# An MLP kernel on one Trainium2 core: w2 casts pinned behind the last GELU, x casts moved, output copies put on ScalarE

## The chip, the cores and the metric

The kernel runs on one core of one Trainium2 chip. The metric is the device time of one execution, in microseconds (us).

Engine names in the profile: PE is TensorE, DVE is VectorE, ACT is ScalarE, POOL is GpSimd, SP is SyncE. A name with q at its end, such as SPq, is the queue of that engine from which DMAs are issued. "L137" is line 137 of the kernel's file. `ps` is a bank, one of the eight buffers into which TensorE accumulates; `tmp` is a temporary on its way out or to VectorE. The DMA share is the mean busy share of the core's 16 DMA engines.

## The reference

```python
x: 8 x 1024 x 1024, w1: 1024 x 4096, w2: 4096 x 1024, all float32
h = x @ w1
h = 0.5 * h * (1 + np.tanh(np.sqrt(2 / np.pi) * (h + 0.044715 * h ** 3)))
return (h @ w2).astype(np.float32)
```

## The kernel before

The 8192 tokens go through in eight superblocks of 1024. Each superblock does two products: `matmul1` with w1 and the GELU, then `matmul2` with w2. Both use a scheme that needs seven block products instead of eight, so that sums of weight blocks are wanted as operands. Operands are 16 bits wide, the inputs are float32 in DRAM.

The first superblock is different from the others, because nothing is prepared yet:

- It loads w1 and w2 in float32 through four staging buffers (`gc`), 512 KB each, 64 loads in all. ScalarE or GpSimd casts each of them to 16 bits, and only then is the buffer free for the next load.
- It keeps the cast w1 blocks in DRAM (`raw_d`). In the second superblock these are loaded again, VectorE makes the sums of w1 from them, and the sums are written to DRAM (`w1_d`) for superblocks three to eight.
- Its second product is done plainly with eight block products (512 matmuls, `matmul2_first`), in two halves of output columns (`b`), each of four quarters (`q`) with four casts (`j`, `a`). Meanwhile VectorE makes the sums of w2 and SyncE writes them to DRAM (`w2_d`), 28 writes of 512 KB.
- The x of the next superblock is cast by DMA from DRAM to DRAM (`x_cast`, on GpSimd's queue), then loaded with a transpose (on SyncE's queue).

SyncE's queue keeps its DMAs in the order of the program (`load_in_order`). On other engines a compile-time scheduler chooses the order. Each engine then runs its instructions in that order. The code is cut, and the comments at the pools are added:

```python
    up = ctx.enter_context(tc.tile_pool(name="up", bufs=26))     # 16-bit operands, "u"
    gcp = ctx.enter_context(tc.tile_pool(name="gcp", bufs=4))    # float32 staging, "gc"
    tp = ctx.enter_context(tc.tile_pool(name="tp", bufs=10))     # temporaries, "tmp"
    pp = ctx.enter_context(tc.tile_pool(name="pp", bufs=8, space=bass.MemoryType.PSUM))
    # ... cut ...
    def cast_in(dst, src, cast):
        st = gcp.tile([P] + list(dst.shape[1:]), F32, name="gc")
        load_in_order(st, src)
        cast(out=dst, in_=st)
    # ... cut: matmul1, with
        def gelu(b, c, src):
            nc.scalar.activation(out=g[b][:, c, :], in_=src, func=GELU)
    # ... cut: in matmul2_first
        for b in range(2):
            banks = [psum() for _ in range(2 * NQ)]
            # ... cut ...
            for q in range(NI // QC):
                raw = raw_units(QC, OH, (b + 1,))
                for j in range(0, QC, 2):
                    c = q * QC + j
                    for a in range(2):
                        cast_in(
                            raw[f"{a + 1}{b + 1}"][:, j:j + 2, :],
                            w2v[b, a, :, c:c + 2, :],
                            pool_copy if b == 0 and q < 2 else nc.scalar.copy,
                        )
                # ... cut: the matmuls of this quarter ...
                if b == 0:
                    keep.append(raw)
                    if q == 0:
                        keep_w1()
                    elif q == 1:
                        xb = x_cast(1, pool_last[0])
                else:
                    # ... cut: the sums of w2 ...
                    if q in (1, 2):
                        write(q - 1)
            if b == 1:
                blocks = x_transpose(xb, load_in_order)
                write(2)
                write(3)
            for i in range(2 * NQ):
                for c in range(NI - TAIL, NI):
                    mm(i, c, ready[c])
                o = temp()
                if i % 2:
                    nc.scalar.copy(out=o, in_=banks[i])
                else:
                    nc.vector.tensor_copy(out=o, in_=banks[i])
                last = store(sb, f"{i // NQ + 1}{b + 1}", i % NQ, o)
```

Of the kernel before, what the change touches and what calls it, by code (L numbers as in the profile page):

```python
# [11 lines left out]
GELU = mybir.ActivationFunctionType.Gelu_apprx_tanh  # L12
# [41 lines left out]
def kernel(  # L54
# [7 lines left out]
    nc = tc.nc  # L62
# [34 lines left out]
    def psum():  # L97
        return pp.tile([P, HT], F32, name="ps")

    def temp():  # L100
        return tp.tile([P, HT], F32, name="tmp")

    def unit(rows, cols):
        return up.tile([P, rows, cols], DT, name="u")

    def tt(out, in0, in1, op):
        nc.vector.tensor_tensor(out=out, in0=in0, in1=in1, op=op)  # L107

    def flat(t):
        return t.rearrange("p a b -> p (a b)")  # L110
# [3 lines left out]
    def load_in_order(out, in_, **kw):  # L114
        return tc.keep_in_program_order(nc.sync.dma_start(out=out, in_=in_, **kw))  # L115
# [8 lines left out]
    def make_sum(ops, m, raw, rows, cols, sl=slice(None)):  # L124

        u, op, v = B_TERMS[m]
        if op is None:
            ops[m] = raw[u]
            return
        if m not in ops:  # L130
            ops[m] = unit(rows, cols)
        tt(ops[m][:, :, sl], raw[u][:, :, sl], raw[v][:, :, sl], op)

    def cast_in(dst, src, cast):
        st = gcp.tile([P] + list(dst.shape[1:]), F32, name="gc")
        load_in_order(st, src)
        cast(out=dst, in_=st)  # L137

    def raw_units(rows, cols, bs=(1, 2)):
        return {f"{a}{b}": unit(rows, cols) for b in bs for a in (2, 1)}  # L140
# [53 lines left out]
    def load_ops(d, ms, rows, cols):  # L194
        ops = {}
        for m in ms:
            t = unit(rows, cols)
            nc.sync.dma_start(out=flat(t), in_=d[:, m - 1, :])
            ops[m] = t
        return ops  # L200
# [70 lines left out]
    def matmul1(xs, sb):  # L271
        g = {b: gp.tile([P, NI, HT], GT, name=f"g{b}") for b in ("11", "12", "21", "22")}

        def product(bank, w, m, first, last):
            ops, cs = w
            for k in range(KH):
                nc.tensor.matmul(  # L277
                    bank,
                    lhsT=ops[m][:, k, cs],
                    rhs=xs[m][:, k, :],  # L280
                    start=(first and k == 0),
                    stop=(k == KH - 1),
                    skip_group_check=not first,
                )

        def gelu(b, c, src):
            nc.scalar.activation(out=g[b][:, c, :], in_=src, func=GELU)  # L287

        late = None

        def finish(c, w, q, s2):
            product(q, w, 6, False, True)
            c22 = temp()
            tt(c22, q, s2, ADD)
            gelu("22", c, c22)

        quads = []

        def ahead(q, step):

            if q == NI // QC:
                return
            if sb > 1:
                if step == 0:
                    quads.append(load_ops(w1_d[q], (4, 5, 1, 2, 3, 7, 6), KH, QW))
                return
            if step == 0:
                quad = MadeQuad(q, sb == 0)
                quads.append(quad)
                if sb == 0:  # L310
                    quad.load()
                    quads[q - 1].keep_raw()
            for m in ((), (4,), (1, 3), (7, 6))[step]:
                quads[q].sum(m)
            if sb == 1 and step == 3:
                quads[q].copy_plain()

        if sb == 0:
            quads.append(MadeQuad(0, True))
            xs.make(5)  # L320
            cs = quads[0].load_cols(0, 1)
            quads[0].sum(4, cs)
            for m in (1, 3, 7, 6):
                if m != 3:
                    xs.make(m)
                quads[0].sum(m, cs)
            for c, n in ((1, 1), (2, 2)):
                cs = quads[0].load_cols(c, n)
                for m in SUMS:
                    quads[0].sum(m, cs)  # L330
        else:
            for step in range(QC):
                ahead(0, step)

        for c in range(NI):
            q, j = divmod(c, QC)
            if j == 0:
                ahead(q + 1, 0)
            w = (quads[q] if sb > 1 else quads[q].ops, slice(j * P, (j + 1) * P))
            pb, qb = psum(), psum()  # L340
            product(pb, w, 4, True, False)
            v = temp()
            nc.scalar.copy(out=v, in_=pb)  # L343
            product(qb, w, 5, True, False)
            u = temp()
            tt(u, v, qb, SUB)
            if late is not None:
                finish(*late)
            rb = psum()
            product(rb, w, 1, True, False)  # L350
            s = temp()
            tt(s, u, rb, ADD)
            product(pb, w, 2, False, True)
            gelu("21", c, pb)
            s2 = temp()
            tt(s2, s, pb, SUB)
            product(qb, w, 3, False, False)
            gelu("12", c, qb)
            product(rb, w, 7, False, True)
            c11 = temp()  # L360
            tt(c11, u, rb, ADD)
            gelu("11", c, c11)
            late = (c, w, qb, s2)
            if j:
                ahead(q + 1, j)
        finish(*late)
        return g, quads[-1]
# [9 lines left out]
    def matmul2_first(sb, g, keep_w1):  # L377


        TAIL = 3  # L380
        keep = []
        made = []
        blocks = None

        def write(q):
            for m in SUMS + PLAIN:
                load_in_order(w2_d[q][:, m - 1, :], flat(made[q][m]))

        for b in range(2):
            banks = [psum() for _ in range(2 * NQ)]  # L390
            ready = []

            def mm(i, c, w):
                for a in range(2):
                    nc.tensor.matmul(  # L395
                        banks[i],
                        lhsT=g[f"{i // NQ + 1}{a + 1}"][:, c, (i % NQ) * P:(i % NQ + 1) * P],
                        rhs=w[a],
                        start=(c == 0 and a == 0),
                        stop=(c == NI - 1 and a == 1),  # L400
# [7 lines that stand above are left out]
                        cast_in(  # L408
                            raw[f"{a + 1}{b + 1}"][:, j:j + 2, :],
                            w2v[b, a, :, c:c + 2, :],  # L410
                            pool_copy if b == 0 and q < 2 else nc.scalar.copy,
                        )
                for j in range(QC):
                    w = [raw[f"{a + 1}{b + 1}"][:, j, :] for a in range(2)]
                    ready.append(w)
                    if q * QC + j < NI - TAIL:
                        for i in range(2 * NQ):
                            mm(i, q * QC + j, w)
                if b == 0:
                    keep.append(raw)  # L420
                    if q == 0:
                        keep_w1()
                    elif q == 1:
                        xb = x_cast(1, pool_last[0])
                else:
                    ops = {}
                    for m in SUMS + PLAIN:
                        make_sum(ops, m, {**keep[q], **raw}, QC, OH)
                    made.append(ops)
# [7 lines that stand above are left out]
                for c in range(NI - TAIL, NI):  # L437
                    mm(i, c, ready[c])
                o = temp()
                if i % 2:  # L440
                    nc.scalar.copy(out=o, in_=banks[i])  # L441
                else:
                    nc.vector.tensor_copy(out=o, in_=banks[i])  # L443
                last = store(sb, f"{i // NQ + 1}{b + 1}", i % NQ, o)
        return last, blocks

# [58 lines left out]
    for sb in range(NSB):  # L505
        g, quad = matmul1(xs, sb)
# [39 lines left out]
```

## Time and profile before

| | before |
|---|---|
| time, median of 3 runs | 1606.53 us |
| TensorE busy | 1578.2 of 1603.7 us |
| first superblock's 960 matmuls on TensorE | 18.3 to 245.7 us |
| any later half superblock | 448 matmuls in 96.69 us |
| DMA busy share, 0 to 246 us | 0.98 |

These are lines of the profile's page of the kernel before: TensorE's busy time, then the busy tenths of TensorE and of the DMA engines and the GB/s that they moved in 40 equal slices of the span (40 us each), and the chain of work that ended last.

```profile
PE 1578.2 (98%) x7296; PEld 717.9 (45%) x7296; DVE 819.6 (51%) x1047; ACT 472.3 (29%) x784; POOL 132.1 (8%) x228
...
PE   7989999999999999999999999999999999999999
...
DMA  9999998674566646546574565746557464544511
GB/s 306 345 316 361 276 397 280 179 288 146 197 188 184 236 171 228 157 153 262 186 221 144 169 238 197 227 131 226 201 203 246 102 265 158 210 157 178 216 53 53
...
PE 95%; DMA 3%; DVE 1%; ACT 1%; issue 0%; SPq 0%; POOL 0%; DVEq 0%
```

TensorE is nearly always busy. In the first six slices, the first superblock, the DMA engines are full as well (9 means 90% or more). After that they are about half busy. The kernel thus has two stages with different limits: in the first, two resources are full at once.

TensorE's waits over 1 us that the change aims at, in the view of waits (what waited, for whom, total us, times, longest us):

```profile
PE ps L277 <- ACT g_216 L287: 7.7, 2, 7.4
...
PE ps L395 <- DVE tmp L443: 3.3, 1, 3.3
```

The first lies at 115.8 to 123.2 us, before the end of the first product. The timeline of ScalarE shows its cause (start, duration, instruction, and in brackets the idle time before it and what ended that):

```profile
110.19 0.58 ACT L343 COPY tmp<-ps 128x512 f32<-128x512 f32 x1
118.76 1.04 ACT L137 CAST u<-gc 128x1024 f16<-128x1024 f32 x1 [8.00 <-DMA gc<-in_w_dram]
...
121.56 0.62 ACT L287 ACTIVATE g_218<-tmp 128x512 bf16<-128x512 f32 x1
...
122.56 0.59 ACT L287 ACTIVATE g_216<-ps 128x512 bf16<-128x512 f32 x1
```

ScalarE stands 8.00 us before a cast of w2 whose load has not landed, and the GELUs queue behind that cast. The second product starts on TensorE at 130.34 us. The second wait is before 191.7 us, at the boundary of the column halves; VectorE's timeline shows it:

```profile
189.80 1.23 DVE L107 TENSOR_TENSOR u<-u 128x2048 f16<-128x2048 f16 x1 [7.20 <-DMA u<-xb]
190.95 0.68 DVE L443 COPY tmp<-ps 128x512 f32<-128x512 f32 x1
```

An output copy (L443) stands behind a sum that waits 7.20 us for the transposed x. TensorE needs the bank that this copy frees.

The timeline of SyncE's load queue (x20 is a run of twenty DMAs, the second column how long the issuing took):

```profile
89.33 44.96 SPq L115 DMA_DIRECT2D gc<-in_w_dram  x20
134.34 7.31 SPq L115 DMA_DIRECT2D w_d_85<-u  x7
...
160.05 26.67 SPq L115 DMA_TRANSPOSE u<-xb  x16
...
202.99 4.79 SPq L152 DMA_DIRECT2D u<-raw_d_81  x4
```

w2 loads go out until 134, then the writes of w2's sums, loads, the transposes of x (27 us), and at 202.99 the reload of w1 for the second superblock. VectorE's timeline has the first sum of that reload at 213.41; TensorE's first matmul of the second superblock comes at 245.73, 32 us later.

```profile
213.41 7.09 DVE L107 TENSOR_TENSOR u<-u 128x2048 f16<-128x2048 f16 x6 [17.25 <-DMA u<-raw_d_81]
```

Last, busy time by engine in three windows, with the granted clock, the DMA share and GB/s as the last three columns:

```profile
85.00:125.00 40.00, 32.59 (x148) 14.55 (x147) 18.82 (x27) 20.59 (x33) 13.18 (x16) 0.93 0.98 317
105.00:124.00 19.00, 11.59 (x53) 5.05 (x51) 5.48 (x9) 9.87 (x15) 2.58 (x6) 0.88 1.00 285
0.00:246.00 246.00, 224.40 (x1026) 104.40 (x1027) 135.45 (x168) 94.25 (x140) 48.42 (x69) 0.97 0.98 332
```

### The profile page before, as it was taken

The page shows a single profiled execution, that of the slowest core. Times are in us where ns is not written, and L with a number is a line of the kernel's source. Part 1 is how long each engine was busy: PE and PEld are TensorE (multiplying, and loading weights), DVE is VectorE, ACT ScalarE, POOL GpSimd, SP SyncE. Part 2 cuts the span into 40 slices and gives each one's busy share as a digit, 9 for nine tenths or more (in the row PEclk, how much of TensorE's full clock was granted, in tenths as well). Part 3 has the DMA queues.
Part 4 walks back from the last instruction along what each step waited for, and adds up shares of the span by engine and source line. Part 5 has one row for each costly group of instructions (what it writes and reads, how often), then busy time and mean ns, then how long its engine had stood idle before and what let it go on. Part 6 is the DMA issues. An engine that isn't in the chain of part 4 may idle for free.

```text
span 1603.7 us, 18985 instructions
## 1 busy us (share of the span) xinstructions
PE 1578.2 (98%) x7296; PEld 717.9 (45%) x7296; DVE 819.6 (51%) x1047; ACT 472.3 (29%) x784; POOL 132.1 (8%) x228
## 2 busy tenths in 40 slices
PE   7989999999999999999999999999999999999999
PEld 4434444444444444444444444444444444444444
DVE  6855336644455444555445554456534555455433
ACT  4645104431044210441114410244103431044310
POOL 2230113001100012000120000100001000000000
PEclk9999999999999999999999999999999999999999
DMA  9999998674566646546574565746557464544511
GB/s 306 345 316 361 276 397 280 179 288 146 197 188 184 236 171 228 157 153 262 186 221 144 169 238 197 227 131 226 201 203 246 102 265 158 210 157 178 216 53 53
DMA packets 161820, 338.91 MB, mean 211 GB/s; under 512 B 72257, under 2 KB 78401, under 8 KB 160833
## 3 DMA queue, kind: packets, MB, share of 16 engines
q1 hardware_dynamic: 146944, 278.97, 50.4%
q0 software_dynamic: 14784, 58.73, 11.5%
q8 instruction: 57, 0.93, 0.2%
q14 instruction: 35, 0.28, 0.1%
HBM read 266.34 MB, written 85.98 MB: 220 GB/s over the span
## 4 chain that ended last, share of the span: by engine, by line
PE 95%; DMA 3%; DVE 1%; ACT 1%; issue 0%; SPq 0%; POOL 0%; DVEq 0%
PE ps L277 46%; PE ps L461 42%; PE ps L395 7%; DMA gc<-in_w_dram 2%; DVE u L107 1%; ACT u L137 0%; DVE tmp L107 0%; DMA u<-in_x_dram 0%; DMA u<-xb 0%; SPq L115 0%; POOL u L118 0%; ACT g_218 L287 0%; ACT g_216 L287 0%; ACT g_217 L287 0%; ACT tmp L343 0%
## 5 line engine op out<-in xcount | busy, mean ns | idle before, releaser
L277 PE MATMUL ps<-u 128*128 128x512 f16 x3584 | 779.8, 380 | 13.1 <-ACT g_216 L287 7.7
L107 DVE TENSOR_TENSOR tmp<-tmp,ps 128x512 f32<-128x512 f32 x652 | 447.1, 687 | 661.6 <-PE ps L461 333.3
L277 PEld LDWEIGHTS <-u 128*128 128x128 f16 x3584 | 351.1, 98 | 440.3 <-issue 15.9
L461 PE MATMUL ps<-u,gc 128*128 128x512 f16 x2240 | 485.7, 379 | 0.0
L461 PEld LDWEIGHTS <-gc 128*128 128x128 bf16 x2240 | 219.2, 98 | 264.3
L375 POOL DMA_DIRECT2D out_dram<-tmp x112 | 60.6, 542 | 1108.0 <-ACT tmp L481 733.9
L107 DVE TENSOR_TENSOR u<-u 128x2048 f16<-128x2048 f16 (+2 forms) x110 | 123.0, 1152 | 56.6 <-ACT u L137 21.5
L343 ACT COPY tmp<-ps 128x512 f32<-128x512 f32 x128 | 73.0, 570 | 258.2 <-PE ps L277 258.2
L107 DVE TENSOR_TENSOR tmp<-ps,tmp 128x512 f32<-128x512 f32 x128 | 88.4, 691 | 5.9 <-PE ps L277 1.2
L481 ACT COPY tmp<-ps 128x512 f32<-128x512 f32 x28 | 16.4, 586 | 177.3 <-PE ps L461 177.3
L395 PE MATMUL ps<-u,g_217 128*128 128x512 f16 x128 | 49.0, 383 | 3.3 <-DVE tmp L443 3.3
L395 PE MATMUL ps<-u,g_218 128*128 128x512 f16 x128 | 49.0, 383 | 0.0
L395 PE MATMUL ps<-u,g_215 128*128 128x512 f16 x128 | 48.9, 382 | 0.0
L395 PE MATMUL ps<-u,g_216 128*128 128x512 f16 x128 | 48.8, 381 | 0.0
L137 ACT CAST u<-gc 128x1024 f16<-128x1024 f32 x36 | 37.2, 1044 | 37.6 <-DMA gc<-in_w_dram 37.6
L487 ACT COPY tmp<-ps 128x512 f32<-128x512 f32 x28 | 16.4, 586 | 80.3 <-PE ps L461 80.3
L475 ACT COPY tmp<-ps 128x512 f32<-128x512 f32 x28 | 16.4, 586 | 74.9 <-PE ps L461 74.9
L118 POOL CAST u<-gc 128x1024 f16<-128x1024 f32 (+1 forms) x26 | 28.5, 1105 | 73.8 <-DMA gc<-in_w_dram 60.0
L254 POOL DMA_DIRECT2D xb<-in_x_dram x56 | 27.5, 509 | 18.1 <-DMA out_dram<-tmp 14.5
L441 ACT COPY tmp<-ps 128x512 f32<-128x512 f32 x8 | 4.7, 586 | 71.1 <-PE ps L395 71.1
L395 PEld LDWEIGHTS <-g_218 128*128 128x128 bf16 x128 | 12.6, 98 | 18.8 <-issue 3.9
L395 PEld LDWEIGHTS <-g_215 128*128 128x128 bf16 x128 | 12.6, 99 | 15.5 <-issue 0.8
(120 smaller groups left out, 848.8 us busy)
## 6 DMA issues: line engine op xcount, KB each, us to landing
gc<-in_w_dram SPq DMA_DIRECT2D x64, 512.0 KB, 6.8
out_dram<-tmp POOLq DMA_DIRECT2D x112, 256.0 KB, 4.4
u<-w_d_85 SPq DMA_DIRECT2D x49, 512.0 KB, 6.4
u<-w_d_86 SPq DMA_DIRECT2D x49, 512.0 KB, 7.1
u<-w_d_87 SPq DMA_DIRECT2D x49, 512.0 KB, 5.8
u<-w_d_88 SPq DMA_DIRECT2D x49, 512.0 KB, 6.3
u<-w_d_77 SPq DMA_DIRECT2D x42, 512.0 KB, 4.8
u<-w_d_78 SPq DMA_DIRECT2D x42, 512.0 KB, 5.1
```

What stands on the lines that cost most here:

```text
L107: nc.vector.tensor_tensor(out=out, in0=in0, in1=in1, op=op)
L118: pool_last[0] = nc.gpsimd.tensor_copy(out=out, in_=in_)
L137: cast(out=dst, in_=st)
L254: nc.gpsimd.dma_start(out=xb[q:q + P, :], in_=x2[s * SB + q:s * SB + q + P, :])
L277: nc.tensor.matmul(bank, lhsT=ops[m][:, k, cs], rhs=xs[m][:, k, :], start=(first and k == 0), stop=(k == KH - 1), skip_group_check=not first,)
L343: nc.scalar.copy(out=v, in_=pb)
L375: return queue.dma_start(out=out2[r0:r0 + P, o0:o0 + OH], in_=src)
L395: nc.tensor.matmul(banks[i], lhsT=g[f"{i // NQ + 1}{a + 1}"][:, c, (i % NQ) * P:(i % NQ + 1) * P], rhs=w[a], start=(c == 0 and a == 0), st ...
L461: nc.tensor.matmul(banks[q], lhsT=a[:, c, :], rhs=pieces[c // QC][:, c % QC, :], start=(first and c == 0), stop=(c == NI - 1), skip_group_ ...
L475: nc.scalar.copy(out=v[q], in_=ps)
L481: nc.scalar.copy(out=c21, in_=ps)
L487: nc.scalar.copy(out=c12, in_=ps)
```

## The change

The intent is to remove both TensorE waits. Every ScalarE cast of w2 is pinned behind the last GELU of the first superblock, so that no cast can stand among the GELUs. In the first half only the first quarter's four casts stay on GpSimd (before: two quarters, eight casts), and in the second half every other pair is on GpSimd, so GpSimd's casts of w2 go from 8 to 12 and ScalarE's from 24 to 20. The x casts follow the last GpSimd cast of the first half, which is now an earlier one. The output copies of the first superblock are all on ScalarE.

```diff
+    def act_late_copy(out, in_):
+        with tc.issue_after(gelu_last[0].ins):
+            nc.scalar.copy(out=out, in_=in_)
+
+    gelu_last = [None]
@@
         def gelu(b, c, src):
-            nc.scalar.activation(out=g[b][:, c, :], in_=src, func=GELU)
+            gelu_last[0] = nc.scalar.activation(out=g[b][:, c, :], in_=src, func=GELU)
@@
-                            pool_copy if b == 0 and q < 2 else nc.scalar.copy,
+                            pool_copy if (q == 0 if b == 0 else j) else act_late_copy,
@@
                     if q == 0:
                         keep_w1()
-                    elif q == 1:
+                    elif q == 3:
                         xb = x_cast(1, pool_last[0])
@@
                 o = temp()
-                if i % 2:
-                    nc.scalar.copy(out=o, in_=banks[i])
-                else:
-                    nc.vector.tensor_copy(out=o, in_=banks[i])
+                nc.scalar.copy(out=o, in_=banks[i])
```

## The prediction

> **What bounds the kernel.** TensorE: busy 1578.2 of 1603.7 us (the page's first part), and 95% of the chain of waits. From 245.9 us on, every half superblock takes 96.69 us for 448 matmuls (0.2158 us each) without a gap. Only the first superblock can be shortened: its 960 matmuls need 207.2 us at that pace but run from 28.1 to 245.9, 217.8 us.
>
> **Where those microseconds are (TensorE's waits, timeline, windows).**
> (1) From 115.8 to 123.2 us TensorE waits 7.4 us for a GELU. ScalarE stands still for 8.0 us, in order, before a w2 cast whose load has not landed (w2 loads issued then take 13.1 us to land, while eight copies of x to fp16 run), with GELUs behind it. Then the granted clock is down (0.71 and 0.84 in the two windows around it). The last 24 matmuls, worth 5.2 us, end at 130.3: 9.3 us lost. The skill, "TensorE: Matmul & The Clock Gate", Part 1, says that an idle window of about 3.4 us lowers the clock and about as much busy time restores it; the trace agrees.
> (2) Around 188 us: 3.3 us idle between the column halves of the second product. VectorE waits 7.2 us for the transposed x with an output copy queued behind it. Clock 0.81. The 512 matmuls from 130.34 to 245.89 take 5.0 us more than 110.5.
> Together 14.3 us, 0.9%.
>
> **What the change does.** No matmul, byte or cast is removed. ScalarE's w2 casts (1.04 us each) go from 24 to 20, GpSimd's (same length) from 8 to 12; the first half has 4 on GpSimd and 12 on ScalarE, these all behind the last GELU. So no cast can block a GELU: (1) should vanish. The 8 output copies of VectorE (0.69 us) go to ScalarE (0.59 us), so VectorE's wait for x cannot hold a bank: (2) should shrink. A bank finishes every 1.3 us; ScalarE keeps up.
>
> **What it costs.** With four staging buffers, w2 loading stops after eight loads until the last GELU at about 122.5 us. The x copies start earlier, about 93 instead of 103.5, and fill part of the hole. Then 16 loads must pass before the first write of sums, at my estimate 6 us for four (512 KB at about 400 GB/s plus casts): that write starts near 143 instead of 134.3, everything behind it on the load queue about 9 us later, while TensorE is 9 us earlier. Weights are cast from 123 on and needed at 135: fine. VectorE's sums for the next superblock began at 213.4, now near 222; TensorE needs them near 232: thin. Also, the last casts of the second half (165.8 to 169.7) move to about 175; output copies are now wanted from 167. If ScalarE's order has casts first, TensorE waits 1 to 3 us at the half boundary, which replaces (2).
>
> **Prediction.** 1606.5 - 9.3 - 5.0 + about 2 for the new wait = 1594 us; 8 in 10 within 1590.5 to 1600. Faster by over 2%: 0.01; within 2%: 0.98; slower by over 2%: 0.01.
>
> **What would show it.** No TensorE wait for a GELU above 1 us after 50 us; first product ending near 121 instead of 130.3; no w2 cast among the GELUs; DMA share clearly under 0.9 between 108 and 122; first write of sums near 143; the second superblock's first matmul 12 to 14 us earlier, near 232 to 234; then 96.69 us per half.
>
> **What would make it wrong.** ScalarE's order might put output copies ahead of casts that the load queue depends on, so that the reload for the second superblock is late and TensorE waits there; or a long wait at the half boundary.

## More of the kernel before

Every number quoted as a time is a median of several executions.

A quad is one of the four quarters in which w1 is loaded.

The stores of the outputs, the x casts and the writes of w1's sums all go through GpSimd's queue.

## The result, and the profile after

| | before | after |
|---|---|---|
| time, median of 4 runs each, same rounds | 1607.14 us (1605.8 to 1608.67) | 1611.15 us (1610.33 to 1612.48) |
| second product of superblock 1 starts | 130.34 us | 119.54 us |
| reload of w1 is issued | 202.99 us | 219.57 us |
| superblock 2 starts on TensorE | 245.73 us | 230.04 us |
| its first product (448 matmuls) ends | 342.60 us | 347.29 us |

The ratio is 1.0025, with a 95% interval from 1.0008 to 1.0043: within 2%, but slightly slower, where 0.8% faster was predicted. A ratio here and below is the mean time of one kernel's fast runs over that of the other's fast runs of the same rounds, so it is not quite the ratio of the medians quoted. From 347.29 us on the profile of after goes at the pace of before, so the whole difference arises before that point: the first product ends 4.7 us later, and the medians differ by 4.0 us.

The same lines of the page, after:

```profile
PE 1578.4 (98%) x7296; PEld 716.6 (45%) x7296; DVE 815.3 (51%) x1039; ACT 474.4 (29%) x788; POOL 136.2 (8%) x232
...
PE   7999988999999999999999999999999999999998
...
DMA  9978999674566645556474465745557464644511
GB/s 319 338 231 314 277 353 390 190 291 149 206 209 183 236 170 210 167 161 261 165 232 146 155 257 190 220 141 215 204 203 251 98 266 164 210 157 174 219 53 53
...
PE 91%; DMA 4%; SPq 2%; DVE 2%; issue 1%; ACT 0%; POOL 0%; DVEq 0%; POOLq 0%
```

TensorE's busy time has not changed. Its row dips in slices 6 and 7 (201 to 281 us) instead of in slice 3, and DMA has lost its nines in slices 3 and 4: 7 and 8, with 231 GB/s in the slice from 80 to 121 us that had 316. TensorE's waits:

```profile
PE ps L284 <- DVE tmp L107: 15.5, 5, 8.4
...
PE ps L284 <- ACT tmp L350: 1.4, 1, 1.4
```

Both waits of before are gone from this view, and a new one, for temporaries written by VectorE, costs 15.5 us. ScalarE goes from its last GELU directly into four casts, as intended:

```profile
120.46 0.63 ACT L294 ACTIVATE g_218<-tmp 128x512 bf16<-128x512 f32 x1 [0.24 <-DVE tmp L107]
121.00 3.87 ACT L137 CAST u<-gc 128x1024 f16<-128x1024 f32 x4
```

The price of that stands in the windows. Between 85 and 125 us the DMA engines were busy 0.65 of the time instead of 0.98, and between 105 and 124 us only 0.23 instead of 1.00:

```profile
85.00:125.00 40.00, 40.00 (x187) 18.14 (x186) 23.15 (x33) 21.50 (x34) 8.35 (x12) 1.00 0.65 204
105.00:124.00 19.00, 19.00 (x90) 8.60 (x88) 10.09 (x14) 11.21 (x18) 0.00 (x0) 1.00 0.23 63
0.00:246.00 246.00, 227.32 (x1051) 106.48 (x1052) 133.56 (x162) 98.97 (x147) 48.44 (x65) 0.98 0.91 308
```

With four staging buffers and every cast but the first quarter's four held back, the w2 loads stop once the buffers are full. Up to 246 us, 308 GB/s moved 75.8 MB, against 81.7 MB before (GB/s times 246 us); after reaches 81.6 MB only at 260 us, 14 us later. That fits the size of the hole: 0.35 of 40 us is 14.0 us of idle DMA. The load queue shows the delay passing through:

```profile
88.05 58.87 SPq L115 DMA_DIRECT2D gc<-in_w_dram  x20
146.97 7.84 SPq L115 DMA_DIRECT2D w_d_85<-u  x7
...
171.99 31.59 SPq L115 DMA_TRANSPOSE u<-xb  x16
...
219.57 4.29 SPq L159 DMA_DIRECT2D u<-raw_d_81  x4
```

The first write of w2's sums is 12.6 us later than before, the transposes are 11.9 us later (and take 31.6 us instead of 26.7), the reload of w1 16.6 us later. TensorE, meanwhile, is 15.7 us earlier. This is TensorE's timeline where the two meet:

```profile
230.04 3.62 PE L284 MATMUL ps<-u 128*128 128x512 f16 x16
242.03 7.08 PE L284 MATMUL ps<-u 128*128 128x512 f16 x24 [8.37 <-DVE tmp L107]
250.50 1.89 PE L284 MATMUL ps<-u 128*128 128x512 f16 x8 [1.39 <-ACT tmp L350]
253.76 23.56 PE L284 MATMUL ps<-u 128*128 128x512 f16 x108 [1.37 <-DVE tmp L107]
281.90 18.28 PE L284 MATMUL ps<-u 128*128 128x512 f16 x73 [4.58 <-DVE tmp L107]
```

The second superblock starts without a wait at 230.04, runs 16 matmuls, and then stops 8.37 us. The 24 matmuls after that take 7.08 us, where 24 at 0.2158 us (96.69 us over 448) are 5.2. The page "TensorE: Matmul & The Clock Gate" of the Trainium skill, Part 1, says that an idle window of about 3.4 us lowers the clock and that about as much busy time restores it; this trace agrees with the pattern: the granted clock was 0.74 between 242 and 249 us. Three more waits follow. From 230.04 to 347.29 are 117.25 us, 20.6 more than the 96.69 that the product needs. In what follows, this excess is called "lost".

Who was late? VectorE's timeline:

```profile
228.42 2.54 DVE L107 TENSOR_TENSOR u<-u 128x2048 f16<-128x2048 f16 x2 [17.31 <-DMA u<-raw_d_81]
...
243.35 0.69 DVE L107 TENSOR_TENSOR tmp<-tmp,ps 128x512 f32<-128x512 f32 x1 [0.24 <-DMA out_dram<-tmp]
...
248.43 0.69 DVE L107 TENSOR_TENSOR tmp<-tmp,ps 128x512 f32<-128x512 f32 x1 [2.65 <-DMA out_dram<-tmp]
...
279.42 1.23 DVE L107 TENSOR_TENSOR u<-u 128x2048 f16<-128x2048 f16 x1 [6.80 <-DMA u<-raw_d_84]
```

It waits 17.31 us for the first block of the reload, and gets to the first sum at 228.42, 1.6 us before TensorE needs it, not 32 us as before. At 243.35 and 248.43 it waits for a temporary that an output store still holds, and at 279.42 it has waited 6.80 us for the fourth quad of w1. GpSimd's queue, which issues the stores, is in the same squeeze:

```profile
228.83 0.54 POOL L199 DMA_DIRECT2D w_d_77<-u  x1 [40.28 <-DMA u<-raw_d_81]
...
231.78 1.08 POOL L382 DMA_DIRECT2D out_dram<-tmp  x2
...
233.59 1.07 POOL L382 DMA_DIRECT2D out_dram<-tmp  x2
237.45 0.54 POOL L382 DMA_DIRECT2D out_dram<-tmp  x1 [2.79 <-DMA w_d_77<-u]
```

The writes of w1's sums (`w_d_77`) come at 228.83 after waiting for the reload, and only then and between further writes come the output stores, the last of them at 245.09. Everything that the second superblock needs from DRAM is late at once.

### The profile page after: what moved, and what is told of

Read it like the earlier page. It is cut to its first block, busy times and chain, and to the rows that moved or that the text cites. A ratio compares the mean times of both kernels' runs of the same rounds, so it can differ in the third digit from the quotient of the medians.

```text
span 1608.6 us, 18983 instructions
## 1 busy us (share of the span) xinstructions
PE 1578.4 (98%) x7296; PEld 716.6 (45%) x7296; DVE 815.3 (51%) x1039; ACT 474.4 (29%) x788; POOL 136.2 (8%) x232
## 4 chain that ended last, share of the span: by engine, by line
PE 91%; DMA 4%; SPq 2%; DVE 2%; issue 1%; ACT 0%; POOL 0%; DVEq 0%; POOLq 0%
PE ps L284 45%; PE ps L465 42%; PE ps L402 3%; SPq L115 2%; DMA gc<-in_w_dram 1%; DVE u L107 1%; DMA u<-raw_d_84 1%; DVE tmp L107 1%; DMA w_d_77<-u 1%; DMA out_dram<-tmp 1%; DMA u<-raw_d_81 0%; DMA u<-in_x_dram 0%; DMA u<-xb 0%; SPq L159 0%; POOL u L118 0%
## 5 line engine op out<-in xcount | busy, mean ns | idle before, releaser
L284 PE MATMUL ps<-u 128*128 128x512 f16 x3584 | 782.2, 381 | 21.4 <-DVE tmp L107 15.5
L350 ACT COPY tmp<-ps 128x512 f32<-128x512 f32 x128 | 72.9, 570 | 264.1 <-PE ps L284 258.7
L485 ACT COPY tmp<-ps 128x512 f32<-128x512 f32 x28 | 16.4, 585 | 177.3 <-PE ps L465 177.3
L118 POOL CAST u<-gc 128x1024 f16<-128x1024 f32 (+1 forms) x30 | 32.5, 1086 | 142.3 <-DMA gc<-in_w_dram 125.3
L491 ACT COPY tmp<-ps 128x512 f32<-128x512 f32 x28 | 16.4, 585 | 80.3 <-PE ps L465 80.3
L479 ACT COPY tmp<-ps 128x512 f32<-128x512 f32 x28 | 16.4, 585 | 74.9 <-PE ps L465 74.9
L137 ACT CAST u<-gc 128x1024 f16<-128x1024 f32 x20 | 20.6, 1044 | 34.1 <-DMA gc<-in_w_dram 34.1
L447 ACT COPY tmp<-ps 128x512 f32<-128x512 f32 x16 | 9.4, 585 | 45.8 <-PE ps L402 45.8
```

The lines of the kernel that those rows point to most:

```text
L118: pool_last[0] = nc.gpsimd.tensor_copy(out=out, in_=in_)
L137: nc.scalar.copy(out=out, in_=in_)
L284: nc.tensor.matmul(bank, lhsT=ops[m][:, k, cs], rhs=xs[m][:, k, :], start=(first and k == 0), stop=(k == KH - 1), skip_group_check=not first,)
L350: nc.scalar.copy(out=v, in_=pb)
L479: nc.scalar.copy(out=v[q], in_=ps)
L485: nc.scalar.copy(out=c21, in_=ps)
```

## The experiments

Fourteen kernels were run. The main theory (A) was that the DMA hole made by the pin delays w1's reload and thus the second superblock. Its rivals were that the ScalarE output copies or the order of the queues (stores behind writes on GpSimd's queue, reload behind writes on SyncE's) are to blame. In the tables, "start" is TensorE's first matmul of the second superblock, "reload" the issue of the first w1 reload, "share" the DMA busy share between 85 and 125 us. Single profiles give these, and even a part that no edit touches moves from profile to profile: the first matmul of the first product came between 17.1 and 18.3 us. The times are medians of 4 to 6 runs, and each ratio is to before. The medians of before were 1606.56 (e1 to e4), 1605.89 (e5 to e8), 1605.9 (e9 to e12) and 1606.42 us (e13, e14).

| run | time, us | ratio [95%] | share | reload | start | lost |
|---|---|---|---|---|---|---|
| before | 1607.14 | 1 | 0.98 | 203.0 | 245.7 | 0.2 |
| after | 1611.15 | 1.0025 [1.0008, 1.0043] | 0.65 | 219.6 | 230.0 | 20.6 |
| e1_copies_only | 1607.99 | 1.0009 [0.9997, 1.0022] | 0.97 | 204.8 | 242.2 | 6.3 |
| e2_pin_only | 1607.66 | 1.0013 [1.0, 1.0025] | 0.83 | 212.8 | 231.2 | 16.6 |
| e3_first_half_gpsimd | 1603.0 | 0.9983 [0.9971, 0.9996] | 0.96 | 203.4 | 231.4 | 12.0 |
| e4_writes_other_queue | 1617.35 | 1.0072 [1.0059, 1.0086] | 0.64 | 222.0 | 236.4 | 21.5 |
| e5_gpsimd_casts_stores_scalar | 1599.37 | 0.9959 [0.9947, 0.9972] | 0.95 | 205.7 | 234.0 | 5.7 |
| e6_after_stores_scalar | 1614.73 | 1.0054 [1.0041, 1.0066] | 0.68 | 221.4 | 232.8 | 23.3 |
| e7_before_stores_scalar | 1606.75 | 1.0005 [0.9993, 1.0018] | 0.96 | 204.6 | 245.7 | 1.6 |
| e8_copies_stores_scalar | 1611.25 | 1.0039 [1.0025, 1.0053] | 0.97 | 205.3 | 243.3 | 6.8 |
| e9_after_fewer_bytes | 1604.9 | 0.9993 [0.998, 1.0006] | 0.62 | 211.1 | 230.9 | 16.2 |
| e10_gpsimd_fewer_bytes | 1592.92 | 0.992 [0.9906, 0.9933] | 0.99 | 189.4 | 231.3 | 0.2 |
| e11_before_more_bytes | 1608.96 | 1.0019 [1.0006, 1.0033] | 0.97 | 213.8 | 245.2 | 3.7 |
| e12_best_try | 1598.27 | 0.9951 [0.9938, 0.9965] | 0.94 | 204.4 | 233.6 | 5.3 |
| e13_x_copies_late | 1621.65 | 1.009 [1.0076, 1.0104] | 0.42 | 233.3 | 243.5 | 20.6 |
| e14_two_quarters | 1605.09 | 0.9994 [0.9981, 1.0007] | 0.82 | 212.9 | 233.0 | 12.4 |

In e13 another wait of 8.58 us, for VectorE's sums, stands before the start, and "lost" does not count it. All kernels gave right results except e9 and e10, which are wrong.

### e1: only the output copies

The kernel before with this edit:

```diff
-                if i % 2:
-                    nc.scalar.copy(out=o, in_=banks[i])
-                else:
-                    nc.vector.tensor_copy(out=o, in_=banks[i])
+                nc.scalar.copy(out=o, in_=banks[i])
```

> The kernel before with the output copies on ScalarE alone. Theory A (late loads: the pinned casts stop the w2 loads, so the reload of w1 for the second superblock comes late): this part is harmless, the 3.3 us wait between the halves and its 1.7 us of slow clock go, the GELU wait of 7.4 us stays; 4 to 5 us faster than before, about 1602. Rival B (the copies on ScalarE and the new queue orders cause the loss): same as before or slower, with waits of TensorE behind 245 us. Rival C (the first superblock is bound by DMA bandwidth, so anything gained early is lost at the start of the second): under 2 us of gain.

Measured: 1607.99 us, no gain. The wait at the half boundary is gone and the second superblock starts 3.5 us earlier, at 242.2. Then its first product loses 6.3 us. GpSimd's timeline shows where the stores stand:

```profile
240.19 0.53 POOL L192 DMA_DIRECT2D w_d<-u  x1 [8.70 <-DMA u<-raw_d]
242.67 0.53 POOL L192 DMA_DIRECT2D w_d<-u  x1 [1.95 <-DMA u<-raw_d]
243.19 3.73 POOL L375 DMA_DIRECT2D out_dram<-tmp  x7
```

Seven output stores come at 243.19, behind two writes of w1 that waited 8.70 and 1.95 us for the reload. The temporaries stay occupied that long. Theory A had expected a gain to stay; it was a miss. It is a first sign that an earlier TensorE can be paid back at the second superblock, even without a hole.

### e2: only the pin

The kernel before with the pin, GpSimd's eight casts kept:

```diff
-                            pool_copy if b == 0 and q < 2 else nc.scalar.copy,
+                            pool_copy if b == 0 and q < 2 else act_late_copy,
```

> The kernel before with the pin alone: GpSimd keeps its eight w2 casts, the other 24 are behind the last GELU. Theory A: the GELU wait vanishes, the DMA share shows a hole before the last GELU, but shorter than after the change since eight loads more than four pass before it; the load of w1 for the second superblock is issued 4 to 12 us later than at 203; part of the gain is lost at the start of the second superblock and at the half boundary; 1600 to 1608. Rival B: all of the GELU gain stays, about 1597. Rival C: 1605 to 1609.

Measured: 1607.66 us. The GELU wait is gone (second product at 119.75), the hole is half as deep as after's (share 0.83), the reload comes at 212.8, and 16.6 us are lost at the second superblock. The wait at the half boundary went too, although half of the copies stayed on VectorE: 0.8 us were left, for a copy of ScalarE. So the second superblock started 14.6 us earlier with the pin alone, and all of it was given back.

### e3: no pinned cast in the first half

The kernel after, with all 16 casts of the first half on GpSimd, so that none of them waits for the last GELU:

```diff
-                            pool_copy if (q == 0 if b == 0 else j) else act_late_copy,
+                            pool_copy if (True if b == 0 else j) else act_late_copy,
```

> The kernel after with all 16 first-half w2 casts on GpSimd (x copies thereby after the 16th), the second half and the output copies as after. No ScalarE cast then stands before the last GELU and none is needed for the first half's loads. Theory A: DMA has no hole between 105 and 121, the w1 reload is issued near 203 or sooner, TensorE has no wait of over 2 us after 45 us; about 13 us faster than before, 1592 to 1596. Rival B: still 1605 or more. Rival C: 1602 or more, with waits at the start of the second superblock although there is no hole.

Measured: 1603.0 us, ratio 0.9983. That is 0.42 points below after's ratio, 6.7 us of 1606. The hole is closed, the reload is back at 203.4, and TensorE is still early:

```profile
85.00:125.00 40.00, 39.43 (x184) 17.80 (x183) 24.66 (x34) 19.85 (x33) 22.14 (x25) 1.00 0.96 317
```

But 12.0 us are still lost:

```profile
231.37 3.62 PE L284 MATMUL ps<-u 128*128 128x512 f16 x16
236.25 1.02 PE L284 MATMUL ps<-u 128*128 128x512 f16 x4 [1.27 <-DVE tmp L107]
246.10 54.24 PE L284 MATMUL ps<-u 128*128 128x512 f16 x243 [8.82 <-DVE tmp L107]
```

So the hole is a cause, worth some 7 to 9 us here (6.7 by the ratios; lost 20.6 against 12.0), and not the only one. Theory A had expected 1592 to 1596 and missed. A TensorE that is 14 us earlier meets a DMA side that is only as early as before.

### e4: part of the writes on another queue

The kernel after, with the last 14 writes of w2's sums on ScalarE's queue, so that they do not stand before the reload on SyncE's:

```diff
             for m in SUMS + PLAIN:
-                load_in_order(w2_d[q][:, m - 1, :], flat(made[q][m]))
+                if q < 2:
+                    load_in_order(w2_d[q][:, m - 1, :], flat(made[q][m]))
+                else:
+                    nc.scalar.dma_start(out=w2_d[q][:, m - 1, :], in_=flat(made[q][m]))
```

> The kernel after with the last 14 writes of w2 sums issued from ScalarE's DMA queue, so that the w1 reload does not stand behind their 16 us of issue; the hole stays. Theory A (order on the serial load queue): the w1 reload is issued 10 to 16 us sooner than 219.6, the 20 us of waits at the start of the second superblock shrink to under 6; 1594 to 1600. Rival C (bandwidth): the reload is issued sooner but lands no sooner than 222, time 1605 or more. Rival B: 1607 or more, since copies and stores keep their engines.

Measured: 1617.35 us, 0.5 points slower than after. The reload went out at 222.0, later and not sooner: SyncE's queue waited 19.7 us for writes of w2 between 150 and 225 us, and ScalarE itself stood behind writes, so that TensorE waited 2.9 us for one of its copies. The Trainium skill, "Trainium Kernel Development and Optimization", Key Constraints, says that DMAs from the SyncE, ScalarE and GpSimd queues run on the same 16 engines and that several issuers save issue time alone. This run agrees in that another queue brought nothing. As a test of A it is confounded, since it put new waits on ScalarE.

### e5, e6, e7: the stores away from GpSimd's queue

The same edit on three kernels: e3 (giving e5), after (e6) and before (e7). The output stores of the first superblock go on ScalarE's queue, and the x casts of the third superblock, which followed the last store, are held at their old place by a mark on a write of w1.

```diff
-        queue = nc.gpsimd if sb < NSB - 1 else nc.sync
+        queue = nc.scalar if sb == 0 else nc.gpsimd if sb < NSB - 1 else nc.sync
@@
-                nc.gpsimd.dma_start(out=w1_d[self.q][:, m - 1, :], in_=flat(self.ops[m]))
+                ins = nc.gpsimd.dma_start(out=w1_d[self.q][:, m - 1, :], in_=flat(self.ops[m]))
+                if self.q == 2 and x_mark[0] is None:
+                    x_mark[0] = ins
@@
-                blocks = x_transpose(x_cast(sb + 1, last), nc.sync.dma_start)
+                blocks = x_transpose(x_cast(sb + 1, x_mark[0] if sb == 1 else last), nc.sync.dma_start)
```

> The kernel of e3 (first-half casts all on GpSimd, no hole), and the output stores of the first superblock issued from ScalarE's DMA queue behind the copies that fill them, so that they no longer stand behind w1 writes on GpSimd's queue that wait for a load; the x copies of the third superblock keep their place on GpSimd's queue. Theory D (in e3 the early TensorE waits 8.8 us because temporaries are held by output stores that stand in order behind those writes): the waits of TensorE on VectorE near 236 to 246 fall from 11.6 to under 4 us; 6 to 10 us faster than e3, 1593 to 1597. Rival C (DMA bandwidth): stores are issued sooner but land late, waits stay over 8 us; 1600 to 1604.

> The kernel after with only the stores of the first superblock moved as in e5; the hole in the w2 loads stays. Theory A and D together: the w1 reload is still issued near 219 and still late, so TensorE still waits for sums behind late loads, but not for temporaries; about 4 to 8 us faster than after, 1603 to 1607, and 8 to 12 us slower than e5, which is what the hole costs. If the hole cost nothing (order of stores alone): equal to e5 within 2 us. If the stores cost nothing: 1611.

> Control: the kernel before with only the stores of the first superblock moved. Before, TensorE reached the second superblock late and waited for no temporary there, so all theories expect the same time as before within 2 us, 1605 to 1608; the wait between the halves may change by 1 us either way.

Measured: e7 1606.75 us, the same as before, as expected of the control. e6 1614.73 us, slower than after by 0.3 points where 1603 to 1607 was expected: with the hole, moving the stores did not help. But e5 and e6 differ only in the casts of the first half, as e3 and after do, and e6 is 15.4 us slower: that is what the hole costs, with all that follows from it, when the stores are off GpSimd's queue. e5 1599.37 us, 0.24 points better than e3: without the hole they did, by about 4 us. The waits of TensorE for VectorE's temporaries went from 11.6 us in e3 to 4.0, but 2.6 us of waits for ScalarE's temporaries appeared, so e5 missed its 1593 to 1597. The order of stores is a second cause, of a few us, and not the main one of after's loss.

### e8: the copies and the stores

e1 with the edit of e5:

> The kernel of e1 (before with the output copies on ScalarE) with the stores of the first superblock moved too. Theory D: e1 won 5 us between the halves and lost it again at the start of the second superblock to the order on GpSimd's queue; so now the 5 us stay, 1600 to 1603. Rival C (bandwidth): 1605 to 1608 as e1.

Measured: 1611.25 us. It was a miss; the store move took nothing off e1's 6.3 us (lost 6.8), and the run is 0.3 points slower than e1. Stores took 14.02 us of the chain of waits. Why it is worse than e1, by some 3 us of the medians, stays open.

### e9 and e10: fewer bytes

After (e9) and e3 (e10) without the last seven writes of w2's sums, 3.67 MB. The result is wrong (the reads of that quarter are pointed at the third one, so that no uninitialized memory is read).

```diff
         def write(q):
+            if q == NI // QC - 1:
+                return
@@
-            pieces = [load_ops(d, (m,), QC, OH)[m] for d in w2_d]
+            pieces = [load_ops(d, (m,), QC, OH)[m] for d in w2_d[:-1] + w2_d[-2:-1]]
```

> The kernel after without the last seven writes of w2 sums (3.67 MB, about 9 us of DMA at the measured 390 GB/s); later superblocks read the third quarter's sums twice, so the result is wrong on purpose; everything TensorE does stays. Theory C (all of the first superblock's traffic, about 82 MB, must pass at the DMA engines' pace before TensorE can go on undisturbed; the change left the DMA engines idle for some 14 us and so pushed the end of this traffic back): 8 to 12 us faster than after, about 1600 to 1603. If only the order of the queues caused the loss and not the traffic: under 4 us faster.

> The kernel of e3 (no hole) without the same seven writes, wrong result on purpose. Theory C: e3 lost 12 us at the start of the second superblock because TensorE arrived 14 us earlier than the traffic was done; 9 us less traffic leaves 2 to 5 us of it: 1592 to 1596. If e3's wait is not traffic: 1600 to 1603.

Measured: e9 1604.9 us, 6.2 us below after (5 by the ratios). That lies between the 8 to 12 expected of traffic and the under 4 expected of queue order, so it decides nothing. e10 1592.92 us, as expected: the reload goes out at 189.4 and the second superblock runs through, 318 matmuls without a gap in the window shown:

```profile
231.30 68.98 PE L284 MATMUL ps<-u 128*128 128x512 f16 x318
```

This is the kernel that I had predicted after to be: both waits gone and nothing given back, at 1593 us. It needed the same removal of waits, no hole, and 3.67 MB less to move. The seven writes also stand just before the reload on SyncE's queue; leaving them out frees the queue some 9 us earlier too, so these two runs do not tell bytes from the place in the queue. And of the 14.0 us by which e10's reload is earlier than e3's, 5.0 were there before the removed writes mattered (the third seven writes began at 182.41 instead of 187.43).

### e11: more bytes in the kernel before

The kernel before with those seven writes done twice, the second time to scratch:

```diff
+            if q == NI // QC - 1:
+                for m in SUMS + PLAIN:
+                    load_in_order(w2_x[:, m - 1, :], flat(made[q][m]))
```

> The kernel before with the last seven writes of w2 sums made twice, the second time to a scratch tensor that nobody reads: 3.67 MB and about 9 us more of DMA, nothing else. Theory C says that the kernel before had almost no slack against its traffic (in e3 about 2 us): 5 to 9 us slower than before, 1611 to 1616. My prediction had given it some 30 us of slack at the first sum: same as before within 1 us.

Measured: 1608.96 us, 3.0 us slower, less than the expected 5 to 9. The reload is 10.8 us later, and 3.7 us are lost. So the kernel before had 7 to 8 us of slack between its DMA side and its TensorE (an estimate: 10.8 minus the 3.7 lost, or minus the 3.0 by which the time grew). Take it with care: the scheduler put e11's output stores behind 10 writes of w1 on GpSimd's queue instead of 16, so more than bytes changed. And e1, with the order of before, lost 6.3 us when the two sides came only 5.4 us closer (start 3.5 earlier, reload 1.8 later). In any case the slack is not the 32 us that the early first sum suggests, and after moves the two sides together by 32 (15.7 earlier on one, 16.6 later on the other).

### e12: a better version

e3, with the second half's stores on ScalarE's queue and the x casts of the third superblock behind the last write of w1:

```diff
-        queue = nc.gpsimd if sb < NSB - 1 else nc.sync
+        queue = nc.scalar if sb == 0 and b[1] == "2" else nc.gpsimd if sb < NSB - 1 else nc.sync
@@
+                if self.q == NI // QC - 1:
+                    x_mark[0] = ins
```

> A version meant to be faster: e3 with only the second half's output stores on ScalarE's queue, and the x copies of the third superblock (6.3 MB read and written at 245 to 256 us) put behind the last w1 write near 290, where the DMA share is 0.7. Theory C: less traffic competes at 245 to 275, so the last waits go: 1593 to 1598, 1 to 6 us faster than e5's 1599.4. If not traffic: as e5 or e3, 1599 to 1603.

Measured: 1598.27 us, correct, 0.49% faster than before and the lowest median of a correct version here. It is just above its expected 1593 to 1598, and 1.1 us below e5, whose runs overlap with it, so it is not shown to beat e5. 5.3 us are still lost at the second superblock.

### e13 and e14: the size of the hole

The first twelve runs left open whether the loss follows the idle time of the DMA engines or the place of the stores and writes in their queues. Two kernels change the hole's depth with after's other parts kept. e13 moves after's x casts, which fill part of the hole, behind the first GpSimd casts of the second half (at 148.8 us instead of 92.9), which makes the hole deeper. e14 gives GpSimd two quarters of the first half, which makes it shallower.

```diff
# e13
-                    elif q == 3:
-                        xb = x_cast(1, pool_last[0])
@@
                     made.append(ops)
+                    if q == 0:
+                        xb = x_cast(1, pool_last[0])
# e14
-                            pool_copy if (q == 0 if b == 0 else j) else act_late_copy,
+                            pool_copy if (q < 2 if b == 0 else j) else act_late_copy,
```

> The kernel after with the eight x copies taken out of the idle stretch: they follow the first two GpSimd casts of the second half, near 145 us, instead of starting at 93. All other queue orders stay nearly as after. If the idle DMA stretch is the cause: it grows by the 10 to 12 us that the x copies filled, the w1 reload is issued 5 to 12 us later than 219.6, and the time rises to 1616 to 1623. If the queue orders are the cause: 1610 to 1613, as after.

> The kernel after with the first two quarters of the first half's casts on GpSimd (eight instead of four), so that four more loads pass before the last GELU: the idle DMA stretch is about 5 us shorter. If it is the cause: the w1 reload is issued 4 to 7 us sooner than 219.6 and the time is 2 to 5 us below after, 1606 to 1609, between after and e3. If the queue orders are the cause: 1610 to 1613, as after.

Measured: e13 1621.65 us, within its expectation; e14 1605.09 us, slightly better than expected. The windows line of e13 shows a DMA share of 0.42:

```profile
85.00:125.00 40.00, 39.70 (x185) 17.90 (x184) 25.96 (x36) 19.97 (x34) 4.64 (x4) 1.00 0.42 155
```

Idle DMA time is 40 us times one minus the share. Ordered by it, the four kernels that differ only in the engine of the first half's casts and in when the x casts come (at 116.9, 104.1, 92.9 and 148.8 us) stand so:

| kernel | idle DMA, 85 to 125 us | time | first product of superblock 2 ends |
|---|---|---|---|
| e3 | 1.6 us | 1603.0 us | 340.10 us |
| e14 | 7.2 us | 1605.09 us | 342.05 us |
| after | 14.0 us | 1611.15 us | 347.29 us |
| e13 | 23.2 us | 1621.65 us | 360.72 us |

From end to end, 21.6 us more idle time cost 20.6 us at the end of that product, 18.7 us by the medians and 17.2 us by the ratios to before (e13's profiled run, 1623.77 us, was its slowest). The steps are uneven: 2.0 us for the first 5.6, 5.2 for the next 6.8, 13.4 for the last 9.2. The source of the four differs only as said, but GpSimd's timelines show that the scheduler also moved the eight output stores: they begin behind 15 writes of w1 in e3, 6 in e14 and 3 in after and e13. So the first two steps mix the hole with the order of the stores. The last one does not: after and e13 have the same order there, and 9.2 us more idle time made the kernel 10.4 us slower by the ratios. The loss follows the hole.

## Why the prediction was wrong, point by point

**Right: both waits go.** The wait for the GELU vanished (second product at 119.54; "near 121" was predicted), and no cast stands among the GELUs. The wait at the half boundary vanished as well, for which e1 (copies) and e2 (pin) were each nearly enough alone, and the clock was 1.00 between 85 and 125 us. TensorE reached the second superblock 15.7 us earlier; 12 to 14 was predicted. About 1.1 us of that is luck: the first product began at 17.17 instead of 18.28, which nothing in the change explains. One number of the prediction does not fit its own sum: 217.8 less 207.2 us leaves 10.6 to gain, not 14.3. The 217.8 us count from 28.1 us, when at least 25 of the 960 matmuls had run; for the other 935, about 16 us were lost.

**Right in kind: the hole.** The DMA share between 105 and 124 us is 0.23. But I let the x casts "fill part of the hole" and did not add up what was left of it, 14.0 us.

**Wrong: "about 2 for the new wait".** This is the term of the sum that failed. The prediction placed a wait of 1 to 3 us at the half boundary; there was none. It gave the second superblock nothing; there 20.6 us were lost. Thus 1606.5 − 9.3 − 5.0 + 2 = 1594 would have had to end in + 20.6 rather than + 2, which gives 1612.8, near the measured 1611.15.

**The step behind that term:** "VectorE's sums for the next superblock began at 213.4, now near 222; TensorE needs them near 232: thin." Two things failed in it. The sizes: the first write came at 147.0 rather than 143, where I had taken about 400 GB/s for the loads after the GELU and 287 were measured from 121 to 147 us, and the delay grew along the queue, so the sums came at 228.4 rather than 222. And the criterion: it is not enough that the first sum is there. TensorE did start at 230.04 without a wait, and stopped after 16 matmuls, because the next sums, the output stores that free the temporaries, and the later quads of w1 all came late from the same full DMA engines. Even without the hole (e3), with the reload 28 us ahead of TensorE, 12.0 us were lost; before had 42.7 us of lead and lost 0.2. The lead is the time from the issue of the reload to the start of the second superblock; 0.2 was lost also in e10, with 41.9 us of it. After had 10.5. With 37.4 us e1 already lost 6.3, but e11 lost only 3.7 with 31.4, so no lead can be named at which the loss begins.

**"What would make it wrong" was close.** It named a late reload. It expected it from ScalarE putting output copies ahead of casts. The runs show the hole instead: e3 keeps those copies on ScalarE and takes only the pinned casts of the first half off it, and the reload is back at 203.4 instead of 219.6.

**What I overlooked in the profile.** "Only the first superblock can be shortened" was read off TensorE alone. The page's DMA row stood at 9 for the first six slices. The Trainium skill, "Perfetto Trace Analysis", Optimization Strategy, says that kernels can have several regimes in which the most contended engine changes; this profile agrees, with a DMA share of 0.98 to 246 us and 0.57 after that. Where two resources are full at once, as here, taking waits from one of them need not gain anything: e1 and e2 each removed a wait and gained nothing.

What stays open: how e3's remaining 12.0 us divide between bytes and the order of the stores (e5 takes about 4 us off, e9 and e10 change both bytes and queue), and why e8 is slower than e1. So does the slack of before. The lead does not order the losses here either: e14 with 20.1 us of lead lost 12.4, hardly more than e3 with 27.9.

## What to carry to other kernels

Before counting a removed wait as a gain, look for the next place where the earlier engine meets another resource that is full in the same stage, and ask by how much that one is ahead; count its megabytes up to a given time, not the arrival of the first tile. When the DMA engines are full, do not hold back the instruction that frees the staging buffers of their loads: give the casts to an idle engine instead (GpSimd here, 6.7 us by the ratios). And test a change in its parts: here each part removed a wait and gave the time back later. Where a scheduler chooses the order, compare the queues of the two kernels before you put a difference down to the edit.

## What the Trainium skill lacked or had wrong

- "Perfetto Trace Analysis", Identifying the Most-Contended Engine, advises HBM utilization rather than occupancy to judge DMA (and then a look for the DMA resource that binds), and its Roofline part names about 435 GB/s for the 16 engines as the bound. Here the first superblock moved 332 GB/s, 76% of that, with transposes and DRAM-to-DRAM casts in the mix, while the busy share was 0.98; and idle DMA time cost time (after to e13: 10.4 us for 9.2). From 220 to 240 us, with a share of 1.03 by the view's count, before moved 415 GB/s. In this mix the busy share told that there was little room, and the rate did not.
- No page that I found says what it costs when DMA engines stand idle in a stage in which they are otherwise full. Here 21.6 us more idle time made the kernel end 18.7 us later (e3 against e13, medians).
